# Three small moves in a tuned GEGLU kernel: paired 4 KB stores, an earlier first block of w_down, and late pieces of x through one PSUM bank

## The chip, the core and the metric

The kernel runs on one core of one Trainium2 chip. The metric is the device time of one execution in microseconds (us). Runs of the kernel before agree within 1.4 us in one set.

TensorE (PE in the profile, PEld for its weight loads), VectorE (DVE), ScalarE (ACT), GpSimd (POOL) and the queue that issues most DMAs (SPq) run side by side and wait for each other by semaphores.

## The reference

```python
x: (8, 1024, 1024)   w_gate, w_up: (1024, 4096)   w_down: (4096, 1024)   # float32
gate, up = x @ w_gate, x @ w_up
h = gelu_tanh(gate) * up
out = h @ w_down
```

## The kernel before

It works in float16 with float32 accumulators, in 8 passes of 1024 tokens. Each pass has a gate/up half and a w_down half. Passes 1 to 3 use a two-by-two fast matrix product with 512-column matmuls (7 products per pair of column blocks, 16 pairs to a pass); passes 4 to 8 use a larger scheme with 256-column matmuls, whose gate/up operands ("entries") are built once, in passes 2 and 3, and stored in HBM.

Some words that come again: the w_down half works through w_down in blocks of 1 MB, numbered from 0, with 32 matmuls for each. An "h product" is VectorE's product of gelu(gate) and up out of PSUM, which frees the accumulator banks. s3 is a buffer for one of the sums of h that the w_down half needs; an "s3 sum" fills a quarter of it. The "jam" is the stretch from 227 to 287 us in which DMA is full.

The parts that matter, cut:

```python
A_PARTS = ([8, 11, 12, 13, 16, 18, 22, 24, 25], [9, 10, 14, 15, 17, 19, 20, 21, 23])
# the sums that pass 2 and pass 3 make; entries_of() mixes in three plain copies each

def make_entry(p, q, e):               # in passes 2 and 3, 24 entries for each of 8 quads
    ...
    if n < 8: nc.scalar.activation(four(v), ..., COPY, scale=float(sign))   # plain: ScalarE
    else:     combine(four(v), op, a_node(p, q, a), a_node(p, q, b))        # sum: VectorE
    nc.sync.dma_start(out=wop[q, e // 2, :, e % 2], in_=v)                  # rows of 2 KB
...
            if i == NP - 1:                      # the last pair of pass 1
                at(1, load_d, p, 2 if p else 0)  # first block of w_down
...
        for r in range(4):                       # in the w_down half
            sums["P1", 0, r] = [("s3", "a11", "a21", SUB, r)]   # during block 0
            sums["P1", 1, r] = [("a21", "a21", "a22", ADD, r)]  # during block 1
...
        # first pair of pass 1: banks 5 and 7 hold pieces of x on their way out of the transpose
        x0_cast(0, 0, 1); x0_transpose(0, 0, 1, 5, act)
        x0_cast(0, 1, 1); x0_transpose(0, 1, 1, 7, dve)
        halves(1)
        product(1, 0, 1, 0)                      # accumulates in bank 5
        cast_first(1, 1, c0, dve)
        product(0, 1, 0, 0)
        ...
        cast_first(0, 1, c1)
        cast_first(1, 1, c1, dve)                # waits for the last landing of w_up
        sum_x(1); sum_w(0, 1, 0); sum_w(0, 1, 1); sum_x(2)
        outputs(1, 0); outputs(1, 1)
        sum_x(3); sum_w(0, 1, 2); sum_w(0, 1, 3); sum_x(4)
```

Of the kernel before, what the change touches and what calls it, by code (L numbers as in the profile page):

```python
# [11 lines left out]
ADD = mybir.AluOpType.add  # L12
SUB = mybir.AluOpType.subtract
# [21 lines left out]
A_SUMS = [  # L35
    (8, 'add', 5, 7), (9, 'sub', 6, 0), (10, 'add', 3, 5), (11, 'sub', 2, 0), (12, 'add', 4, 8), (13, 'sub', 1, 11),
    (14, 'sub', 1, 9), (15, 'add', 4, 10), (16, 'add', 4, 5), (17, 'add', 4, 9), (18, 'sub', 13, 3), (19, 'sub', 7, 14),
    (20, 'add', 2, 15), (21, 'add', 0, 1), (22, 'sub', 11, 8), (23, 'sub', 10, 9), (24, 'sub', 8, 1), (25, 'add', 6, 12),
]
# [8 lines left out]
A_ENTRIES = [  # L48
    (9, -1), (3, 1), (2, 1), (15, 1), (16, 1), (8, 1), (23, 1), (11, -1),
    (10, 1), (12, 1), (17, 1), (20, 1), (22, -1), (21, 1), (25, 1), (24, -1),  # L50
    (13, 1), (4, 1), (14, 1), (6, -1), (18, -1), (7, 1), (19, 1), (1, -1),
]
# [7 lines left out]
    (23, 22, 4, False),  # L60
]

A_PARTS = ([8, 11, 12, 13, 16, 18, 22, 24, 25], [9, 10, 14, 15, 17, 19, 20, 21, 23])

AFTER = {
    1: [('snap', 's8', 1)],
# [107 lines left out]
def kernel(  # L174
# [8 lines left out]
    nc = tc.nc  # L183
# [12 lines left out]
    NP = I // P // 2  # L196
    NQ = NP // 2
    G = MH // P
    FAST = 3
# [103 lines left out]
    def x0_cast(mh, gp, kh):  # L303
        nc.vector.tensor_scalar(
            x0_piece(x0_f16, 2 * mh + gp, kh), x0_piece(x0_f32[mh], gp, kh), XSC, None, MUL
        )

    def x0_transpose(mh, gp, kh, b, copy):
        h = x0_piece(x0_f16, 2 * mh + gp, kh)
        ps = ps_all[:, b].bitcast(FP16).rearrange("p (k m) -> p k m", m=MQ)  # L310
        o = xq[f"b{kh + 1}{mh + 1}"][:, :, gp * MQ : (gp + 1) * MQ]
        for k in range(KH):
            for t in range(2):
                nc.tensor.transpose(
                    ps[:, k, t * P : (t + 1) * P], h[:, t, k * P : (k + 1) * P], identity
                )
        copy(o, ps)
# [47 lines left out]
        xc[:, j * 1024 : (j + 1) * 1024] for j in range(8, 12)  # L365
    ]
    turn = [0]

    def four(v):
        return v.rearrange("p (w k n) -> p w k n", w=2, k=KH)  # L370
# [7 lines left out]
    def make_entry(p, q, e):  # L378
        n, sign = A_ENTRIES[e]
        v = place[q, n] = places[turn[0] % len(places)]  # L380
        turn[0] += 1
        if n < 8:
            nc.scalar.activation(four(v), a_node(p, q, n), COPY, scale=float(sign))
        else:
            _, op, a, b = A_SUMS[n - 8]
            combine(four(v), op, a_node(p, q, a), a_node(p, q, b))
        nc.sync.dma_start(out=wop[q, e // 2, :, e % 2], in_=v)

    def entries_of(part):
        sums = [n for n, _, _, _ in A_SUMS if n in A_PARTS[part]]  # L390
        plain = [n for n, _ in A_ENTRIES if n < 8][3 * part : 3 * part + 3]
        nodes = []
        for j, n in enumerate(sums):
            nodes.append(n)
            if j % 3 == 1:
                nodes.append(plain[j // 3])
        ids = [n for n, _ in A_ENTRIES]
        return [ids.index(n) for n in nodes]



# [49 lines left out]
    def half_block(v):  # L451
        lo, hi = slice(0, HH), slice(HH, 2 * HH)
        return (
            wd_half[0][:, :, lo], wd_half[1][:, :, lo], wd_t[1], wd_t[0],
            wd_half[0][:, :, hi], wd_half[1][:, :, hi], wd_half[0][:, :, lo],
        )[v]
# [71 lines left out]
    def d_place(p, k):  # L528
        if p == 0:

            return (4, 2, 3, 5, 4, 5, 4)[k // 2]
        return order[0][k % 6]

    def d_chunk(p, k):
        if p == 0 and k % 2:
            return half_block(k // 2)
        o = 4096 * d_place(p, k)
        return rg[:, o : o + 4096].rearrange("p (n h) -> p n h", n=8)

# [149 lines left out]
    def gate_up_one(p):  # L689
        unit_steps = {}  # L690
        if p in UNITS_ONE:
            free = deque(xc[:, j * 512 : (j + 1) * 512] for j in range(32, 38))
            free.append(spare)
            for u, s0, ds in UNITS_ONE[p]:
                load, fs = wd_unit(u, xc[:, 12288:16384], free)
                unit_steps[s0] = load
                for k, f in enumerate(fs):
                    unit_steps[s0 + 36 + ds * k] = f
        for i in range(NP):
            q, e = divmod(i, 2)  # L700
            extra = {k: [] for k in range(1, 15)}

            def at(k, f, *a):
                extra[k].append(lambda: f(*a))

            if p == 0 and i == 0:
                first_pair()
                continue
            if p == 0:
                if e == 1:  # L710
                    at(13, load_raw, p, q + 2)
                if 11 <= i < 15:
                    at(7, half_load, 0, 2 * (i - 11))
                if i >= 14:
                    at(4, half_load, 1, 4 * (i - 14))
                    at(6, half_load, 1, 4 * (i - 14) + 2)
                for n in range(4):

                    s0 = 28 * n + 72
                    for ds, f, a in (  # L720
                        (0, wd_load, (n, 0)), (2, wd_load, (n, 1)),
                        (4, wd_load, (n, 2)), (6, wd_load, (n, 3)),
                        (22, wd_sums, (0,)), (23, wd_sums, (1,)),
                        (24, wd_sums, (2,)), (25, wd_sums, (3,)), (26, wd_store, (n,)),
                    ):
                        pr, k = divmod(s0 + ds - 1, 14)
                        if pr == i:
                            at(k + 1, f, *a)
            elif i == 0:
                at(1, load_raw, p, 1)  # L730
            elif e == 1:

                at(13, load_raw, p, q + 2)

            ks = (3, 5, 7, 9) if e == 0 else (11, 12, 13, 14)
            for n, k in enumerate(ks):
                at(k, sum_w, p, i + 1, n)

            if FAST - 2 <= p < FAST:
                for j, n in enumerate(entries_of(p - FAST + 2)):  # L740
                    if j // 6 == e:
                        at(2 * (j % 6) + 2, make_entry, p, q, n)
            if (p, i) in ((0, 2), (FAST - 1, 13)):
                at(8, cast_x, p + 1)
            for k in range(14):
                if 14 * i + k in unit_steps:
                    at(k + 1, unit_steps[14 * i + k])
            if i == NP - 2:
                order[0] = [0, 1, 4, 2, 3, 5] if p % 2 == 0 else [2, 3, 4, 0, 1, 5]
                if p:  # L750
                    at(2, load_d, p, 0)
                    at(3, load_d, p, 1)
            if i == NP - 1:
                at(1, load_d, p, 2 if p else 0)
            second = p == 0 and i == 1
            pair(p, i, extra, SEQ0 if second else SEQ, AFTER0 if second else AFTER1)

# [149 lines left out]
    def down(p):  # L907
# [26 lines left out]

        sums = {}
        for r in range(4):
            sums["P1", 0, r] = [("s3", "a11", "a21", SUB, r)]
            sums["P1", 1, r] = [("a21", "a21", "a22", ADD, r)]
            sums["P2", 0, r] = [("a11", "a21", "a11", SUB, r)]
            sums["P6", 0, r] = [("a12", "a12", "a11", SUB, r)]  # L940

# [315 lines left out]
    def first_pair():  # L1257
# [3 lines left out]
        def product(mh, kh, w, j, c=full):  # L1261
            for k in range(KH):
                nc.tensor.matmul(
                    ps_all[:, bank[mh, j, w], c],
                    raw(0, 0)[:, w, kh * KH + k, j * P : (j + 1) * P],
                    xq[f"b{kh + 1}{mh + 1}"][:, k, c],
                    start=(kh == 0 and k == 0 and c.start == 0),
                    stop=(kh == 1 and k == KH - 1),
                    skip_group_check=True,
                )  # L1270
# [43 lines left out]
        for c in (lo, hi):  # L1314
            for j in range(2):
                product(1, 0, 0, j, c)
        x0_cast(0, 0, 1)
        x0_transpose(0, 0, 1, 5, act)
        x0_cast(0, 1, 1)
        x0_transpose(0, 1, 1, 7, dve)  # L1320
        halves(1)
        product(1, 0, 1, 0)
        cast_first(1, 1, c0, dve)
        product(0, 1, 0, 0)
        product(0, 1, 0, 1)
        x0_cast(1, 0, 1)
        x0_transpose(1, 0, 1, 7, act)
        x0_cast(1, 1, 1)
        product(0, 1, 1, 0)
        product(0, 1, 1, 1)  # L1330
        x0_transpose(1, 1, 1, 7, dve)
        outputs(0, 0)
        outputs(0, 1)
        for w in range(2):
# [2 lines left out]
        nc.gpsimd.tensor_copy(mark, staging0(1, 0)[:, 0, 256:257])  # L1337
        load_raw(0, 1)
        for c in (lo, hi):
            for w, j in ((0, 0), (0, 1), (1, 0)):  # L1340
                product(1, 1, w, j, c)
        for kh in range(2):
            product(1, kh, 1, 1)
        cast_first(0, 1, c1)
        cast_first(1, 1, c1, dve)
        ps_free.clear()
# [61 lines left out]
```

## Time and profile before

| | before |
|---|---|
| median, three runs | 2254.71 us |
| span of the profiled run | 2252.9 us |
| TensorE idle in the span | 7.7 us |
| single waits of TensorE in its list | 6, together 4.3 us, the last at 279 us |

The prediction shows the list of waits and the chain. Beside them, three stretches are needed. A timeline has the start in us, the duration, engine, line, operation, output and inputs, shape and count, and in brackets the idle time ahead and who ended it.

TensorE in the first pair: a wait of 0.65 us for ScalarE's copy out of bank 5.

```profile
15.54 1.06 PE L314 MATMUL ps<-identity,h_a 128*128 128x128 f16 x16
17.25 2.10 PE L1263 MATMUL ps<-x_b,ring 128*128 128x512 f16 x9 [0.65 <-ACT x_b L317]
```

VectorE at the beginning of the w_down half of pass 1: sums of s3 and half-sums of w_down (L461), one on the heels of the other.

```profile
214.59 2.35 DVE L932 TENSOR_TENSOR h_s<-h_a,h_a 128x2048 f16<-128x2048 f16 x2
216.86 1.21 DVE L461 TENSOR_TENSOR x_sums<-x_sums 128x2048 f16<-128x2048 f16 x1
218.00 1.21 DVE L932 TENSOR_TENSOR h_a<-h_a,h_a 128x2048 f16<-128x2048 f16 x1
```

The issuing queue ahead of the last wait: four DMA transposes of the next x, then the load of block 10 of w_down, for which TensorE waits.

```profile
259.64 11.07 SPq L255 DMA_TRANSPOSE x_b<-x_half  x4
270.81 0.53 SPq L544 DMA_DIRECT2D ring<-wd_ops  x1
```

### The profile page before, as it was taken

The numbers are of one execution on the slowest core, as the hardware profiler recorded it, in microseconds if no ns is written. First come the engines' busy times: TensorE is split into PE (matmuls) and PEld (weight loads), VectorE is DVE, ScalarE is ACT, GpSimd is POOL, SyncE is SP. The second block draws the span as 40 slices with busy tenths as digits, with TensorE's granted clock in tenths as the row PEclk, the third lists the DMA queues.
The fourth block names the chain that finished last, engine by engine and source line by source line (L and its number), as shares of the span: only waits on it lengthen the run. The fifth ranks groups of instructions, "written<-read, shape, count | busy, mean of one in ns | idle before, by whom it ended". The sixth has DMA issues, their size and how long they took to land.

```text
span 2252.9 us, 42769 instructions
## 1 busy us (share of the span) xinstructions
PE 2245.2 (100%) x16616; PEld 1624.1 (72%) x16616; DVE 1560.6 (69%) x2189; ACT 956.4 (42%) x1863; POOL 680.6 (30%) x825
## 2 busy tenths in 40 slices
PE   9999999999999999999999999999999999999999
PEld 4444444444444445888888888888888888888888
DVE  6666458883588755777776677666776667866674
ACT  4443135651355622666125550356404653055520
POOL 1332013330133200555014550255402543044520
PEclk9999999999999999999999999999999999999999
DMA  9898969989999999999998999989999889988876
GB/s 243 164 209 216 288 180 242 262 267 289 247 227 249 279 311 348 328 350 363 302 337 278 316 300 321 321 270 324 307 327 316 286 308 318 318 315 275 283 289 232
DMA packets 309133, 642.46 MB, mean 285 GB/s; under 512 B 79104, under 2 KB 185344, under 8 KB 288384
## 3 DMA queue, kind: packets, MB, share of 16 engines
q1 hardware_dynamic: 254144, 566.57, 73.5%
q0 software_dynamic: 54784, 73.14, 19.3%
q8 instruction: 130, 2.13, 0.4%
q14 instruction: 75, 0.61, 0.1%
HBM read 574.36 MB, written 138.41 MB: 316 GB/s over the span
## 4 chain that ended last, share of the span: by engine, by line
PE 87%; DMA 2%; SPq 1%; DVE 0%; issue 0%; DVEq 0%
PE ps L857 40%; PE ps L1108 20%; PE ps L635 17%; PE ps L1000 10%; DMA wd_quads<-x_sums 1%; SPq L255 0%; DMA ring<-wd_ops 0%; PE ps L1130 0%; DVE x_sums L278 0%; DVE h_a L932 0%; DVE tmp L1140 0%; SPq L496 0%; DVEq L278 0%; SPq L544 0%
## 5 line engine op out<-in xcount | busy, mean ns | idle before, releaser
L857 PEld LDWEIGHTS <-ring 128*128 128x128 f16 x8320 | 814.1, 98 | 94.4
L834 POOL TENSOR_TENSOR h_a<-tmp 128x256 f16<-128x256 f32 x640 | 469.2, 752 | 839.1 <-ACT tmp L822 831.9
L857 PE MATMUL ps<-x_sums,ring 128*128 128x256 f16 x5760 | 655.8, 273 | 0.0
L819 DVE TENSOR_TENSOR tmp<-tmp,ps 128x512 f32<-128x512 f32 x640 | 414.3, 683 | 148.2 <-PE ps L857 100.7
L635 PEld LDWEIGHTS <-ring 128*128 128x128 f16 x2632 | 257.4, 98 | 311.9 <-issue 1.1
L804 ACT COPY tmp<-ps 128x512 f32<-128x512 f32 x520 | 304.5, 586 | 236.7 <-PE ps L857 164.4
L635 PE MATMUL ps<-x_sums,ring 128*128 128x512 f16 x1504 | 340.1, 379 | 0.6 <-DVE x_sums L267 0.4
L822 ACT ACTIVATE tmp<-tmp 128x256 f32<-128x256 f32 x640 | 264.3, 418 | 172.6 <-DVE tmp L817 79.2
L857 PE MATMUL ps<-x_b,ring 128*128 128x256 f16 x2560 | 305.6, 273 | 0.0
L817 DVE TENSOR_TENSOR tmp<-ps,tmp 128x512 f32<-128x512 f32 x240 | 165.4, 689 | 145.2 <-ACT tmp L804 99.9
L635 PE MATMUL ps<-x_b,ring 128*128 128x512 f16 x1128 | 259.3, 379 | 0.1
L661 POOL TENSOR_TENSOR h_a<-tmp 128x512 f16<-128x512 f32 x94 | 145.5, 1548 | 372.9 <-ACT tmp L659 265.6
L1108 PEld LDWEIGHTS <-h_a 128*128 128x128 f16 x2208 | 216.0, 98 | 25.0
L1000 PE MATMUL ps<-ring,h_a 128*128 128x512 f16 x1024 | 222.3, 379 | 0.7 <-DMA ring<-wd_ops 0.7
L1108 PE MATMUL ps<-ring,h_a 128*128 128x256 f16 x1888 | 212.6, 273 | 0.0
L1000 PEld LDWEIGHTS <-h_a 128*128 128x128 f16 x1152 | 112.7, 98 | 136.8 <-DMA ring<-wd_ops 1.2
L654 DVE TENSOR_TENSOR tmp<-ps,tmp 128x512 f32<-128x512 f32 x188 | 127.2, 684 | 113.7 <-ACT tmp L646 112.2
L1238 ACT ACTIVATE tmp<-ps 128x512 f32<-128x512 f32 x60 | 35.3, 598 | 362.5 <-PE ps L1108 274.5
L1171 DVE SCALAR_TENSOR_TENSOR tmp<-ps,tmp 128x512 f32<-128x512 f32 x119 | 80.4, 690 | 95.0 <-PE ps L1108 64.1
L360 DVE TENSOR_TENSOR ring<-ring 128x1024 f16<-128x1024 f16 x188 | 137.6, 745 | 10.5 <-DMA ring<-in_w_up_dram 6.2
L646 ACT COPY tmp<-ps 128x512 f32<-128x512 f32 x188 | 109.8, 586 | 78.5 <-PE ps L635 78.5
L1108 PE MATMUL ps<-ring,x_sums 128*128 128x256 f16 x1120 | 126.3, 273 | 0.0
(105 smaller groups left out, 1538.0 us busy)
## 6 DMA issues: line engine op xcount, KB each, us to landing
ring<-w_ops SPq DMA_DIRECT2D x480, 512.0 KB, 4.8
ring<-wd_quads SPq DMA_DIRECT2D x110, 1024.0 KB, 7.1
ring<-wd_ops SPq DMA_DIRECT2D x35, 1024.0 KB, 7.9
w_ops<-h_s SPq DMA_DIRECT2D x128, 256.0 KB, 6.7
out_dram<-tmp SPq DMA_DIRECT2D x127, 256.0 KB, 6.3
ring<-in_w_gate_dram POOLq DMA_DIRECT2D x23, 1024.0 KB, 10.4
ring<-in_w_up_dram POOLq DMA_DIRECT2D x23, 1024.0 KB, 18.0
wd_quads<-x_sums SPq DMA_DIRECT2D x131, 128.0 KB, 6.6
```

What stands on the lines that cost most here:

```text
L360: nc.vector.tensor_tensor(o, a, b, op)
L635: nc.tensor.matmul(ps(b, w), lhs[:, k], rhs[:, k, :], start=(first and k == 0), stop=(k == KH - 1), skip_group_check=True,)
L654: nc.vector.tensor_tensor(o, ps("b", w), o, ADD)
L661: nc.gpsimd.tensor_tensor(hq[TO[n]][:, i, :], tmp[:, t[n, 1]], tmp[:, t[n, 0]], MUL)
L804: nc.scalar.copy(tmp[:, t[o[1]]], ps_all[:, bank[o[2]]])
L817: nc.vector.tensor_tensor(d, b, a, SUB)
L819: nc.vector.tensor_tensor(d, a, b, ADD if o[4] == "add" else SUB)
L822: nc.scalar.activation(d, d, GELU, scale=GSC)
L834: nc.gpsimd.tensor_tensor(h, tmp[:, t[o[1]], MQ : 2 * MQ], g, MUL)
L857: nc.tensor.matmul(ps_all[:, bank[c], w * MQ : (w + 1) * MQ], lhs[:, w, k], rhs[:, k], start=(first and w == 0 and k == 0), stop=(k == KH ...
L1000: nc.tensor.matmul(ps_all[:, bank[b, g]], lhs[:, j, g * P : (g + 1) * P], dc[:, n, :], start=(first and j == 0), stop=(j == NP - 1), skip_ ...
L1108: nc.tensor.matmul(ps_all[:, bank[c], m * MQ : (m + 1) * MQ], lhs[:, j, m * P : (m + 1) * P], rhs[:, j, :], start=(first and j == 0 and m ...
```

## The change

Its intent, as one reads it from the diff: fewer and longer stores in passes 2 and 3; w_down's block 0 loaded into s3 while DMA is idle, so that the one ring place that it used is free for block 8; and product work for TensorE while a late piece of x is copied out of PSUM.

```diff
-A_PARTS = ([8, 11, 12, 13, 16, 18, 22, 24, 25], [9, 10, 14, 15, 17, 19, 20, 21, 23])
+A_PARTS = (
+    [16, 8, 11, 12, 22, 21, 25, 24, 13, 4, 18, 7],
+    [9, 3, 10, 23, 2, 15, 17, 20, 14, 6, 19, 1],
+)
 ...                                                   # make_entry: part 1
-        nc.sync.dma_start(out=wop[q, e // 2, :, e % 2], in_=v)
+        if turn[0] % 2 == 0 and e % 2 and made_last[0] == (q, e - 1):
+            ...                                         # both places of the pair
+            nc.sync.dma_start(
+                out=wop[q, e // 2], in_=v.rearrange("p (e n) -> p e n", e=2)
+            )
+        elif (e ^ 1) not in entries_of(0 if p < FAST - 1 else 1):
+            nc.sync.dma_start(out=wop[q, e // 2, :, e % 2], in_=v)
 ...                                                   # part 2
+        if p == 0 and k == 0:
+            return hf["s3"][:, 4096:8192].rearrange("p (n h) -> p n h", n=8)
 ...
             if i == NP - 2:
+                at(2, load_d, p, 0)
                 if p:
-                    at(2, load_d, p, 0)
                     at(3, load_d, p, 1)
-            if i == NP - 1:
-                at(1, load_d, p, 2 if p else 0)
+            if i == NP - 1 and p:
+                at(1, load_d, p, 2)
 ...
-            sums["P1", 0, r] = [("s3", "a11", "a21", SUB, r)]
+            late = p == 0 and r > 1
+            sums.setdefault(("P1", int(late), r % 2 if late else r), []).append(
+                ("s3", "a11", "a21", SUB, r)
+            )
 ...                                                   # part 3
+        product(1, 0, 1, 1)                            # bank 7
         x0_cast(0, 0, 1)
-        x0_transpose(0, 0, 1, 5, act)
         x0_cast(0, 1, 1)
-        x0_transpose(0, 1, 1, 7, dve)
+        x0_transpose(0, 0, 1, 5, dve)
         halves(1)
-        product(1, 0, 1, 0)
+        x0_transpose(0, 1, 1, 5, dve)
 ...                                                   # the next two pieces too go through 5, not 7
```

More of the change, by code (lines that the diff above doesn't have):

```diff
@@ L367 @@
     turn = [0]
+    made_last = [None]
     def four(v):
@@ L386, in make_entry @@
             combine(four(v), op, a_node(p, q, a), a_node(p, q, b))
-        nc.sync.dma_start(out=wop[q, e // 2, :, e % 2], in_=v)
-    def entries_of(part):
-        sums = [n for n, _, _, _ in A_SUMS if n in A_PARTS[part]]
-        plain = [n for n, _ in A_ENTRIES if n < 8][3 * part : 3 * part + 3]
-        nodes = []
-        for j, n in enumerate(sums):
-            nodes.append(n)
-            if j % 3 == 1:
-                nodes.append(plain[j // 3])
+        if turn[0] % 2 == 0 and e % 2 and made_last[0] == (q, e - 1):
+            k = (turn[0] - 2) % len(places)
+            v = hf["s3"][:, k * 1024 : (k + 2) * 1024] if k < 8 else xc[:, k * 1024 : (k + 2) * 1024]
+            nc.sync.dma_start(
[3 more added lines that the diff above has]
+            nc.sync.dma_start(out=wop[q, e // 2, :, e % 2], in_=v)
+        made_last[0] = (q, e)
+    def entries_of(part):
         ids = [n for n, _ in A_ENTRIES]
-        return [ids.index(n) for n in nodes]
+        return [ids.index(n) for n in A_PARTS[part]]
     def wd_load(q, t):
@@ L936, in down @@
         for r in range(4):
-            sums["P1", 0, r] = [("s3", "a11", "a21", SUB, r)]
-            sums["P1", 1, r] = [("a21", "a21", "a22", ADD, r)]
+            late = p == 0 and r > 1
+            sums.setdefault(("P1", int(late), r % 2 if late else r), []).append(
+                ("s3", "a11", "a21", SUB, r)
+            )
+        for r in range(4):
+            sums.setdefault(("P1", 1, r), []).append(("a21", "a21", "a22", ADD, r))
             sums["P2", 0, r] = [("a11", "a21", "a11", SUB, r)]
@@ L1326, in first_pair @@
         x0_cast(1, 0, 1)
-        x0_transpose(1, 0, 1, 7, act)
+        x0_transpose(1, 0, 1, 5, act)
         x0_cast(1, 1, 1)
@@ L1330, in first_pair @@
         product(0, 1, 1, 1)
-        x0_transpose(1, 1, 1, 7, dve)
+        x0_transpose(1, 1, 1, 5, dve)
         outputs(0, 0)
@@ L1339, in first_pair @@
         for c in (lo, hi):
-            for w, j in ((0, 0), (0, 1), (1, 0)):
+            for w, j in ((0, 0), (0, 1), (1, 1)):
                 product(1, 1, w, j, c)
         for kh in range(2):
-            product(1, kh, 1, 1)
+            product(1, kh, 1, 0)
         cast_first(0, 1, c1)
```

## The prediction

> **What bounds the kernel now.** I read the page, then TensorE's list of waits, then the chain of waits in order of time, then timelines of the stretches in which TensorE stops.
>
> From the page, and from the list of waits (engine and line of the waiter, what it waited for; us in total, times, longest):
>
> ```profile
> PE 2245.2 (100%) x16616; PEld 1624.1 (72%) x16616; DVE 1560.6 (69%) x2189; ACT 956.4 (42%) x1863; POOL 680.6 (30%) x825
> ```
>
> ```profile
> PE ps L1284 <- DVE h_s L1287: 1.6, 1, 1.6
> PE ps L314 <- DVE h_a L304: 0.7, 1, 0.7
> PE ps L1000 <- DMA ring<-wd_ops: 0.7, 1, 0.7
> PE ps L1263 <- ACT x_b L317: 0.7, 1, 0.7
> PE ps L635 <- DVE x_sums L267: 0.4, 1, 0.4
> PE ps L635 <- DVE ring L360: 0.2, 1, 0.2
> ```
>
> TensorE is idle for 7.7 us of 2252.9. Six single waits make 4.3 us of it, all before 280 us; the rest is mostly the tail. The chain (start us, duration us, what) goes on without a break from there:
>
> ```profile
> 270.81 8.35 DMA ring<-wd_ops
> ...
> 279.21 27.80 PE ps L1000 x128
> 307.01 193.39 PE ps L635 x896
> 500.39 96.69 PE ps L1000 x448
> 597.09 193.39 PE ps L635 x896
> ```
>
> 193.39 us over 896 matmuls is 215.8 ns for 512 columns, and the later 181.65 us over 1664 is 109.2 ns for 256. The list of waits from 307 us on is empty. So the reader is to see that only the first 307 us can become shorter; everything behind (some 1946 us) can only become longer.
>
> **What the skill says.** "TensorE: Matmul & The Clock Gate", section "Wait — 56ns, not 53.3ns?", gives 215.7 ns between warm matmuls of 512 columns and 55.6 ns for 128. The trace agrees (215.8; the transposes step by 56), so the matmuls themselves hold no slack. "Perfetto Trace Analysis", section "DMA Optimizations", says that DMAs under 2 KB carry an overhead and that 4 KB pieces help. In this trace a 2 KB packet took 90 ns and a 1 KB one 50, so the gain of larger packets is small here, and no matmul waits for these stores. "SBUF — State Buffer", section "Who interferes with whom", says that a VectorE instruction with two SBUF inputs contends with a GpSimd one that reads SBUF. The trace agrees: a 128x2048 sum took 2.29 us beside a GpSimd product and 1.22 without. "Perfetto Trace Analysis", section "Matmuls", wants groups of matmuls to rotate through PSUM banks so that an eviction overlaps the next group; the third part of the change does the opposite.
>
> **Part 1, stores in pairs of 4 KB rows (passes 2 and 3).** Before: 24 entries x 8 quads = 192 stores of 256 KB. After: of each part's 12 entries 10 form five adjacent pairs and two stay single, so 2 x 8 x 5 = 80 stores of 512 KB and 32 of 256 KB: 80 issues fewer, at 0.3 us of the issuing queue each. Nobody waits for them until pass 4. What it moves: pass 2 gets 10 sums and 2 plain copies per quad instead of 9 and 3, and all six entries of its even pairs become VectorE work (before: five). VectorE is already full there:
>
> ```profile
> 355.35:367.44 12.09, 12.09 (x58) 5.49 (x56) 12.09 (x17) 6.70 (x11) 4.66 (x4) 1.00 1.04 225
> ```
>
> (one pair; busy us of TensorE, weight loads, VectorE 12.09 of 12.09, ScalarE, GpSimd, then clock and DMA.) One sum more is 0.6 to 1.1 us before the two products that free the accumulators. The one that matters, the first h product, ends 1.3 us before the next pair's third product needs its bank in this worst pair (367.85, against 367.44 + 8 x 0.216 = 369.17), 1.7 to 2.4 us in the others. So I count 0 for part 1, with little to spare.
>
> **Part 3, the first pair.** Before, TensorE waits 0.65 us at 17.25 for a ScalarE copy of 1.01 us out of bank 5. After, from 15.54 us: a product of four matmuls (0.86) to 16.40; transpose 1 (8 x 56 ns) to 16.85; the VectorE copy starts 0.19 later and takes 0.69, to 17.73; transpose 2, from the same bank, 17.79 to 18.24; its copy to 19.12; next product at 19.18. Before, that product started at 17.25 + 0.86 = 18.11. Same work in both, so TensorE is **1.07 us later**: two waits of some 0.9 us in place of one of 0.65. That delay then meets slack:
>
> ```profile
> 26.80 3.89 PE L635 MATMUL ps<-x_b,ring 128*128 128x512 f16 x16
> 30.53 1.03 PE L635 MATMUL ps<-x_sums,ring 128*128 128x512 f16 x4
> 31.95 2.75 PE L635 MATMUL ps<-x_sums,ring 128*128 128x512 f16 x12 [0.40 <-DVE x_sums L267]
> 34.89 2.13 PE L635 MATMUL ps<-x_sums,ring 128*128 128x512 f16 x9 [0.19 <-DVE ring L360]
> ```
>
> Start-to-start steps above 216 ns here are 0.28 us at 28.80 (a ScalarE copy in PSUM), 0.56 at 31.95 and 0.35 at 34.89: 1.19 us. The last two hang on VectorE, which runs without a break from 27.61, and that start is a landing of w_up at 27.59, behind 8 MB of loads that the change doesn't touch (DMA share 0.99 from 3 to 28 us). So the product at 34.89 starts there as before if the shift is under 1.19. **Net 0, at worst +0.2.** By the same bound, saving the 0.65 altogether would also have given 0.
>
> **Part 2, the first w_down block a pair sooner.** It is loaded from about 187 instead of 197.41 us, a stretch where DMA is nearly idle (0.01 to 0.02 from 185 to 191), into half of s3. Before, it landed at 203.5, and TensorE needed it at 209.31: no wait there, so 0 directly. Block 8 no longer waits for the end of block 0 and is issued at about 210 instead of 216.41; it is needed at 264.56, so 0 again. The price: two of the four s3 sums on VectorE must wait until TensorE has read block 0 (216.3). Before, VectorE went from sum to sum, with both done at 216.94 and a second w_down half-sum at 218.0; after, it has finished what it may do at 215.8, and idles till 216.4. Adding up the listed sums (1.13 each, 0.34 for the small ones), the fourth small sum ends at 225.77 instead of 225.09: **+0.67 us**. Behind it, in order on the same queue, come two stores of 1 MB (226.09 and 226.88). With these a stretch begins in which DMA is full:
>
> ```profile
> 227.00:287.00 60.00, 59.33 (x276) 26.73 (x275) 23.72 (x35) 8.40 (x15) 1.81 (x2) 1.00 1.08 301
> ```
>
> (219 to 227 had a share of 0.49.) At the end of that jam stands the only wait of this stage: block 10, queued behind four DMA transposes of x (11.07 us of issue from 259.64), lands at 279.16, while TensorE was due at 278.37 (step 1052 - 216 = 0.84 us). If the jam starts up to 0.67 us later with the same bytes, and its two weight loads of 1 MB do not shift, block 10 lands 0.3 to 0.7 later: the wait grows from 0.84 to about 1.3. **+0.5 us.**
>
> Sum: 0 + 0.05 + 0.5 on 2254.71 gives 2255.3; I take a little off, as the change was surely made for a gain: **2255.1 us**.
>
> **Rivals.** (a) Sooner loading relieves the queue, and block 10 lands in time. For it: 1 MB leaves the neighbourhood of 216 to 221 us. Against it: that load was over before the jam began. It would give -0.84, some 2253.9. (b) Part 3 does what it seems meant for and TensorE gains 0.65 at 17.25. Against it: the copies are serial in one bank, and VectorE's landing at 27.59 takes any gain back; 2254.7, no change. (c) The extra VectorE sum in the even pairs of pass 2 overruns the 1.3 to 2.4 us and TensorE waits for a bank, 0.3 to 1 us in some of seven pairs: +1 to +4, up to 2259. For it: VectorE at 12.09 of 12.09, and sums stretched to 2 us by GpSimd; against it: one sum more fits on average, and odd pairs have 2 to 4 us free. (d) The jam is chaotic (a store lands 9 us after its issue, and VectorE waits for buffers that stores free), so block 10 may move by 1 us either way.
>
> **Range and chances.** The three runs before spread over 1.4 us. All effects are of that size: (a) at the low end less the spread is 2253.3, (d) or a little of (c) at the high end 2256.9. Range 2253.3 to 2256.9. Two per cent is 45 us, ten times the largest rival: faster 0.005, within 2% 0.99, slower 0.005.
>
> **What would show it.** Right: TensorE's list has two waits on VectorE for bank 5 near 17 and 18.5 us, of 0.7 to 0.9, and nothing left at 31.95; the first product after VectorE's third weight sum still starts at 34.9; block 0 is issued near 187; the wait for block 10 is above 0.8 us; the list is empty from 307 us on; that stretch takes 1946 us as before. Wrong: a wait for block 10 gone or under 0.5 us (a), waits of TensorE on VectorE between 307 and 500 us (c), or a start at 34.9 that moved by over 0.3 us, which would say that VectorE's landing isn't the bound there.

## The result

| | before | the change |
|---|---|---|
| median (range), 6 runs each | 2254.43 us (2253.45 to 2254.88) | 2254.68 us (2253.79 to 2255.3) |
| span of the profiled run | 2252.9 | 2252.7 |

The ratio is 1.0002, with a 95% interval of 0.9989 to 1.0014: the same.

The new list of TensorE's waits:

```profile
PE ps L1298 <- DVE h_s L1301: 1.6, 1, 1.6
PE ps L317 <- DVE h_a L307: 0.9, 2, 0.6
PE ps L1014 <- DMA ring<-wd_ops: 0.9, 1, 0.9
PE ps L317 <- DVE x_b L320: 0.8, 1, 0.8
PE ps L1277 <- DVE x_b L320: 0.8, 1, 0.8
PE ps L1277 <- ACT ring L343: 0.3, 1, 0.3
PE ps L643 <- DVE ring L363: 0.2, 1, 0.2
```

The 0.7 us behind ScalarE's copy is gone; two waits of 0.8 us behind VectorE's copies (x_b, L320) stand in its place, and the wait for block 10 (L1014) is still there. The first pair on TensorE:

```profile
15.69 0.61 PE L317 MATMUL ps<-identity,h_a 128*128 128x128 f16 x8
17.08 0.61 PE L317 MATMUL ps<-identity,h_a 128*128 128x128 f16 x8 [0.78 <-DVE x_b L320]
18.47 1.89 PE L1277 MATMUL ps<-x_b,ring 128*128 128x512 f16 x8 [0.78 <-DVE x_b L320]
```

In this profile the extra product of four begins at 14.82 us, so the product at 18.47 comes 3.65 us after it. In before, the same work began at 15.54 and reached that product at 17.25 + 0.86 = 18.11: 2.57 us. The first pair is 1.08 us longer on TensorE. A little later:

```profile
30.61 3.81 PE L643 MATMUL ps<-x_sums,ring 128*128 128x512 f16 x16
34.60 1.68 PE L643 MATMUL ps<-x_sums,ring 128*128 128x512 f16 x7 [0.19 <-DVE ring L363]
```

The product at 34.60 is the one at 34.89 in before. I call its start **the mark**: the first product on the third weight sum of pair 1. In both profiles it starts 7.30 us after the last landing of w_up (27.59 and 27.30 us). The 1.08 us have gone into the gaps ahead of it.

The chain from the last wait on:

```profile
271.33 7.76 DMA ring<-wd_ops
...
279.13 27.80 PE ps L1014 x128
306.94 193.39 PE ps L643 x896
500.32 96.69 PE ps L1014 x448
```

Behind 307 us it has the same durations as before, and the list of waits from 307 us on is empty again. The stores of part 1 did get fewer: 192 of 256 KB became 80 of 512 KB and 32 of 256 KB. The DMA packets of before and of the change:

```profile
DMA packets 309133, 642.46 MB, mean 285 GB/s; under 512 B 79104, under 2 KB 185344, under 8 KB 288384
```

```profile
DMA packets 297611, 642.44 MB, mean 285 GB/s; under 512 B 77824, under 2 KB 184064, under 8 KB 276864
```

**The span as a sum.** One table holds all 14 profiles. The clock column is the start of the first 512-column matmul that is followed within 230 ns, which tells when TensorE goes from 427 to 216 ns per matmul. (It is read from the spacing, because the clock that the profile prints is 1.00 in the slow stretch too, as in the first 5 us of before. Where transposes come first, they show the step up to 0.4 us earlier.) The wait column is the start-to-start step at block 10, less 216 ns. The last column is the span less the mark, less that wait, less waits behind 307 us (0.31 in p3_only, 21.4 in sums_twice).

| kernel | clock quick at | mark, after last landing of w_up | wait for block 10 | span | rest |
|---|---|---|---|---|---|
| before | 9.59 | 34.89, 7.30 | 0.84 | 2252.9 | 2217.2 |
| p1_only | 6.23 | 34.70, 7.31 | 0.84 | 2252.6 | 2217.1 |
| p2_only | 9.16 | 34.77, 7.30 | 1.37 | 2253.3 | 2217.2 |
| before_unwarmed | 11.46 | 34.72, 7.32 | 0 | 2251.8 | 2217.1 |
| the change | 5.85 | 34.60, 7.30 | 1.05 | 2252.7 | 2217.1 |
| p3_only | 6.16 | 34.68, 7.30 | 0.77 | 2252.9 | 2217.1 |
| after_unwarmed | 9.25 | 34.70, 7.30 | 1.05 | 2252.8 | 2217.1 |
| late_swapped | 10.81 | 35.35, 8.01 | 1.25 | 2253.6 | 2217.0 |
| sums_twice | 10.37 | 35.56, 7.91 | 1.43 | 2275.3 | 2217.0 |
| transposes_later | 5.95 | 34.65, 7.31 | 0 | 2251.7 | 2217.1 |
| late_by_twelve | 5.93 | 36.71, 9.30 | 0.77 | 2254.5 | 2217.0 |
| product_between | 5.99 | 34.62, 7.31 | 0 | 2251.7 | 2217.0 |
| xsums_early | 6.03 | 34.14, 6.69 | 0.54 | 2251.7 | 2217.0 |
| three_together | 10.22 | 34.34, 6.79 | 0 | 2251.4 | 2217.0 |

The rest is the same within 0.3 us in kernels whose spans differ by 24 us. So every span here is that rest plus the mark, plus the wait for block 10, plus what TensorE loses in pass 2. Each experiment is read in these columns; the timed medians differ by little more than their spread.

### The profile page after: what moved, and what is told of

It reads as the page before. It is cut to its first block, busy times and chain, and to the rows that moved or that the text cites. A ratio compares the mean times of both kernels' runs of the same rounds, so it can differ in the third digit from the quotient of the medians.

```text
span 2252.7 us, 42628 instructions
## 1 busy us (share of the span) xinstructions
PE 2244.0 (100%) x16616; PEld 1622.7 (72%) x16616; DVE 1560.8 (69%) x2190; ACT 954.1 (42%) x1862; POOL 677.1 (30%) x825
## 4 chain that ended last, share of the span: by engine, by line
PE 98%; DMA 1%; SPq 1%; DVE 0%; issue 0%; DVEq 0%
PE ps L866 40%; PE ps L643 25%; PE ps L1122 20%; PE ps L1014 13%; DMA h_a<-in_w_up_dram 0%; SPq L337 0%; DMA ring<-wd_ops 0%; SPq L301 0%; PE ps L1144 0%; DVE x_sums L270 0%; DVE ring L363 0%; DVE h_a L1290 0%; DVE ring L343 0%; DVE tmp L1154 0%; DVEq L1290 0%
## 5 line engine op out<-in xcount | busy, mean ns | idle before, releaser
L1014 PE MATMUL ps<-ring,h_a 128*128 128x512 f16 x992 | 215.3, 379 | 0.9 <-DMA ring<-wd_ops 0.9
L1014 PEld LDWEIGHTS <-h_a 128*128 128x128 f16 x1152 | 112.6, 98 | 137.1 <-DMA ring<-wd_ops 1.4
L363 DVE TENSOR_TENSOR ring<-ring 128x1024 f16<-128x1024 f16 x188 | 143.0, 769 | 11.4 <-DMA ring<-in_w_up_dram 7.0
```

The costliest lines, as they stand in the source:

```text
L363: nc.vector.tensor_tensor(o, a, b, op)
L1014: nc.tensor.matmul(ps_all[:, bank[b, g]], lhs[:, j, g * P : (g + 1) * P], dc[:, n, :], start=(first and j == 0), stop=(j == NP - 1), skip_ ...
```

## The experiments

Each kernel was timed beside the kernel before on the same chip. All but sums_twice have 1 in the interval of their ratio. All results were correct.

### Each part alone: p1_only, p2_only, p3_only

The edit is one part of the diff above, put into the kernel before.

> The kernel before with part 1 alone (other order of the entries, stores in pairs). My theory: nobody waits for these stores, and VectorE's extra sum in the even pairs of pass 2 stays inside the slack; time within 0.7 us of before (2254.4), no wait of TensorE after 307 us, smallest gap between the first h product and the matmul that needs its bank 1.2 us or more. Rival (VectorE overruns): waits of 0.3 to 1 us in some even pairs of pass 2, +1 to +4 us. Rival (4 KB packets relieve the queues so that something ends sooner): under 2253. Up to 307 us this kernel is the same as before, so its wait for block 10 also shows how far that wait varies by itself: 0.84 in the profile of before, 1.05 in that of the change.

Measured: 2253.77 us against 2254.92 (ratio 0.9995, interval 0.998 to 1.001), and no wait behind 307 us. The gap between the first h product of an even pair of pass 2 and the third matmul group of the next pair, which takes over its bank, was at least 1.32 us. So no wait, and no relief that reaches TensorE either.

> The kernel before with part 2 alone (first block of w_down into s3 a pair sooner, two s3 sums later). In the profile of the change VectorE did not idle as I had forecast, so my mended theory is: no effect; wait for block 10 between 0.7 and 1.1 us as in a kernel without the part, the step at 34.9 as in before (7.30 us after the last landing of w_up), time within 0.7 us of before. The theory on record: wait about 1.3 us, +0.5. Rival (a), the queue is relieved: wait gone, -0.8.

Measured: 2254.93 us against 2254.92 (0.9999, 0.9983 to 1.0016). The mark is where it was, and the wait for block 10 is 1.37 us, above my mended theory and where the theory on record had put it. One profile can't decide between the two; late_swapped and the other profiles take this up.

> The kernel before with part 3 alone (first pair). Theory: two waits of TensorE on VectorE for bank 5 of about 0.78 us each in place of one of 0.65; TensorE 1.08 us later at the next product (3.65 us from the start of the extra product of four, against 2.57 from the start of the transposes in before), and yet the first product on the third weight sum starts 7.30 us after the last landing of w_up, as in before: net 0. Rival: the delay is carried on, the step is 1 us later against the landing and the time +1. Wait for block 10 as in before, 0.7 to 1.1.

Measured: 2254.67 us against 2254.92 (0.9998, 0.9983 to 1.0013). The two waits are there, 0.78 us each, and the mark lies 7.30 us behind the landing. The theory holds in this profile.

This one, which has pass 2 as in before, also held a surprise: the chain leaves TensorE once in pass 2.

```profile
442.28 0.61 DVE tmp L654
...
442.91 0.28 ACT tmp L659
...
443.45 1.04 ACT h_s L383
444.49 0.48 ACT tmp L646
...
445.01 55.41 PE ps L635 x256
```

A plain copy of an entry on ScalarE (L383) held up a PSUM snapshot (L646), and TensorE lost 0.31 us. But that copy was itself late because VectorE was: from 429.85 to 442.89 us the chain lies on VectorE almost without a break, and the h products of the pair before came 1.4 us later, counted from the start of the pair, than in before. The first of them had only 0.17 us to spare. So the order of entries that the change replaces can itself make TensorE wait. It did so in one of four profiles that have it; none of nine with the new order (sums_twice left out) had such a wait.

### The order of the two late s3 sums: late_swapped

```diff
-            sums.setdefault(("P1", int(late), r % 2 if late else r), []).append(
+            sums.setdefault(("P1", int(late), 3 - r if late else r), []).append(
```

In the change VectorE never idled at this place:

```profile
213.17 2.35 DVE L467 TENSOR_TENSOR x_sums<-x_sums 128x2048 f16<-128x2048 f16 x2
215.44 1.21 DVE L941 TENSOR_TENSOR h_s<-h_a,h_a 128x2048 f16<-128x2048 f16 x1
216.58 1.21 DVE L941 TENSOR_TENSOR h_a<-h_a,h_a 128x2048 f16<-128x2048 f16 x1
```

> The change, with its two late s3 sums in the other order: the one that overwrites the last rows of block 0 first. It has to wait for the very last matmul on block 0, so VectorE should idle 0.6 to 0.9 us here, which is the idle time that my prediction had put into the change itself. What follows tells whether the second half of that step was right: if the jam of the DMA queue starts as much later and block 10 lands later, the wait for block 10 grows from about 1.0 to 1.3 to 1.7 us and the time by 0.3 to 0.7; if the landing is set by something else, the wait stays between 0.8 and 1.1.

```profile
216.90 1.23 DVE L941 TENSOR_TENSOR h_s<-h_a,h_a 128x2048 f16<-128x2048 f16 x1 [0.67 <-issue]
```

Measured: VectorE idles 0.67 us, as expected, and the first 1 MB store of the jam is issued 17.53 us after the start of the w_down half; it is 16.78 in every other profile, to the hundredth. The wait for block 10 is 1.25 us. Its landing, counted from the same start, is 70.27 us. In the other profiles that leave its place in the queue alone it was 69.86, 69.86, 69.79 and 68.62 without part 2, and 70.07, 70.39, 68.55, 69.56, 69.79, 70.45 and 70.07 with it. One profile with 0.75 us more can't be told from a spread of 1.9 us, so whether a later jam makes block 10 land later stays open. What the columns do show is that part 2 isn't clear of that spread: the means of the two sets are 69.53 and 69.84. In all these profiles block 10 is issued 61.0 to 62.3 us after that start, and it lands 6.8 to 9.2 us after its issue; what sets this second time was not found.

The timed median was 2255.67 us against 2254.92 (1.0003, 0.9988 to 1.0018). In its profile the mark, too, came 0.7 us late, before any edit of this kernel could act.

### The place in the queue: transposes_later

```diff
-                    if nb == 0 and g == 0 and p + 1 < NPASS:
+                    if nb == (p == 0) and g == 0 and p + 1 < NPASS:
```

> The change, with the four DMA transposes of x issued behind the load of block 10 in pass 1, not ahead of it. Theory: block 10 is late only because it stands behind these transposes in the issuing queue; it is now issued near 258 to 260 us, lands by 270, the wait (1.05 us in the change's profile) is gone and the time is 0.8 to 1.1 us shorter. Rival: the queue is full anyway and block 10 lands as late, or block 12 takes its place behind the transposes and is waited for: no gain.

The issuing queue, which is to be compared with that of before:

```profile
259.30 0.40 SPq L552 DMA_DIRECT2D ring<-wd_ops  x1
259.74 14.00 SPq L258 DMA_TRANSPOSE x_b<-x_half  x4
```

Measured: block 10 landed at 267.08 us, 12 us sooner, nobody waited for it or for block 12, and the span is 2251.7. The median was 2253.53 us against 2254.12 for before (0.9997, 0.998 to 1.0014): the right direction, but too small for the runs to settle. That the wait comes from block 10's place behind four transposes, and not from the amount of data in the queue, is shown by the landing; the missing wait alone would not show it, since it was 0 by chance in two other profiles.

### Who holds the start: product_between, xsums_early, late_by_twelve

product_between lets the extra product cover the first of the two copies:

```diff
-        product(1, 0, 1, 1)
         x0_cast(0, 0, 1)
 ...
         halves(1)
+        product(1, 0, 1, 1)
         x0_transpose(0, 1, 1, 5, dve)
```

> The change, with the extra product of four matmuls put between the two transposes that share bank 5, so that it covers the first copy. TensorE reaches the next product about 0.78 us sooner (one wait left of two). Theory: no gain, because VectorE, held by the last landing of w_up, is the bound: the first product on the third weight sum still starts 7.3 us after that landing, and the saved 0.78 us comes back as waits just before it. Rival: TensorE's start counts, and the step is 0.5 to 0.8 us sooner against the landing.

```profile
31.68 2.75 PE L643 MATMUL ps<-x_sums,ring 128*128 128x512 f16 x12 [0.15 <-DVE x_sums L270]
34.62 2.56 PE L643 MATMUL ps<-x_sums,ring 128*128 128x512 f16 x11 [0.19 <-DVE ring L363]
```

Measured: one of the two waits is gone, and the mark is 7.31 us behind the landing, as ever. The saved time came back ahead of it. Its span of 2251.7 would look like a gain of 1 us over the change; that is the wait for block 10, which happened to be zero in this profile. The median is 2254.07 us against 2254.12.

xsums_early gives VectorE two sums to do ahead of the cast that waits for the last landing:

```diff
         cast_first(0, 1, c1)
+        sum_x(1)
+        sum_x(2)
         cast_first(1, 1, c1, dve)
 ...
-        sum_x(1)
         sum_w(0, 1, 0)
         sum_w(0, 1, 1)
-        sum_x(2)
```

> The change, with two sums of x (1.13 and 1.22 us) put on VectorE ahead of the cast that waits for the last landing of w_up, into the 2.35 us in which it idles. Theory: VectorE's chain behind the landing is 2.35 us shorter, TensorE no longer waits for it, and the first product on the third weight sum starts 6.7 to 6.8 us after the landing (TensorE's own pace, 7.30 less the waits of 0.19 and 0.35), so 0.5 us are gained. Rival: the bound isn't VectorE's chain: 7.3 as before.

```profile
24.96 1.22 DVE L270 TENSOR_TENSOR x_sums<-x_b,x_b 128x2048 f16<-128x2048 f16 x1
26.21 1.23 DVE L270 TENSOR_TENSOR x_sums<-x_b,x_sums 128x2048 f16<-128x2048 f16 x1
27.47 0.69 DVE L343 CAST ring<-h_a 128x1024 f16<-128x1024 f32 x1
```

Measured: the sums fill the hole exactly, the cast starts with the landing (27.44), and the mark comes 6.69 us after it, 0.61 less than in the change. The median is 2253.69 us against 2254.12 (0.9996, 0.9982 to 1.0011). So the chain landing, cast, sums was the bound; without it TensorE's own pace is.

late_by_twelve delays TensorE by 12 idle matmuls:

```diff
         product(0, 1, 0, 1)
+        for _ in range(12):
+            nc.tensor.matmul(ps_all[:, 5], warm_w, warm_x, start=True, stop=True)
         x0_cast(1, 0, 1)
```

> The change, with 12 idle matmuls of 512 columns (2.59 us) on TensorE in the first pair. Theory: the waits of 0.19 and 0.35 us behind VectorE take up 0.54 and the rest stays: the first product on the third weight sum starts 9.3 to 9.4 us after the last landing of w_up. For block 10: if its landing is tied to TensorE's progress (the jam in front of it begins with work that follows TensorE), the wait stays at 0.8 to 1.1 us and the time grows by about 2.0; if the landing is set by the DMA queues alone, the wait vanishes and the time grows by about 1.0.

Measured: the mark is at 9.30 us, so 2.00 of the 2.59 us came through. The wait for block 10 stayed, 0.77 us, and the median is 2256.24 us against 2254.12. Block 10's landing moves along with TensorE; the wait is no cushion in which a delay of the start could vanish.

### The slack in pass 2: sums_twice

```diff
-            combine(four(v), op, a_node(p, q, a), a_node(p, q, b))
+            for _ in range(2 if p == FAST - 2 and e in entries_of(0)[:6] else 1):
+                combine(four(v), op, a_node(p, q, a), a_node(p, q, b))
```

> The change, with each of the six VectorE sums of an even pair of pass 2 computed twice into the same place (the result stays right). Theory of the slack in pass 2: the first h product now has 1.64 to 2.65 us to spare before the matmul that needs its bank; five more sums of 0.6 us or more (3.0 us and up) ahead of it overrun that, and TensorE waits in most of the eight even pairs, 0.4 to 1.5 us each: +3 to +10 us in all, with waits between 307 and 500 us in the list. It shows that part 1's single extra sum used up some of a real limit. Rival: no such limit here: no wait, time as the change.

The list of waits from 300 us on:

```profile
PE ps L644 <- DVE tmp L663: 9.6, 11, 0.9
PE ps L644 <- DVE h_a L681: 6.3, 7, 1.2
```

Measured: 2276.5 us against 2254.85 (1.0094, 1.0079 to 1.011), double the most that I had expected. Behind 307 us TensorE loses 21.4 us from start to start; the list, which counts from modelled ends, has 16.7 with a third line of 0.8. The limit is real, but I had reckoned pair by pair. The odd pairs didn't empty VectorE's backlog: 48 extra sums at 0.6 us or more are at least 29 us, and VectorE had 193.4 - 158.9 = 34.5 us free in that half of the change. With some of them stretched, VectorE would have become the bound of the pass; this is reckoned, not tested apart. The run shows that a limit is there, not what part 1's one sum uses of it.

### The late clock: before_unwarmed, after_unwarmed

Both leave out the first seven idle matmuls (`warm(7)`).

> The kernel before without its first seven idle matmuls, so that TensorE's step from 427 to 216 ns for a 512-column matmul comes late (in the profiles so far it came at 5.9 to 6.2 us in seven kernels and at 9.2 to 10.8 in five, by chance of the execution). Question: does part 3 cost time when that step is late? With the change's first pair the first product on the third weight sum was 7.30 us after the last landing in the early profiles, but 8.01 and 7.91 in two late ones. Theory: with the first pair of before there is 1.08 us more to spare, so this kernel stays near 7.30, or, if the step comes so late that TensorE is the bound here too, lies 0.7 to 1.1 us under its sister. Rival: the late clock hides it equally, both the same.

> The change without its first seven idle matmuls. Theory: TensorE is the bound in the first pair, so part 3's 1.08 us are no longer hidden: the first product on the third weight sum comes 8 us or more after the last landing of w_up, 0.7 to 1.1 us more than in the sister kernel if the clock steps up at the same time in both, and the kernel is 0.5 to 1 us slower than it. Rival: 7.3 in both, same time.

Measured: 2254.3 us (0.9999, 0.9986 to 1.0013) and 2254.99 us (1.0001, 0.9989 to 1.0014), both against 2254.86. The quick clock came at 11.46 us in the first and at 9.25 us in the second, so the pair didn't meet under the same clock, and my forecast of 8 us or more for the second missed. Yet the two profiles are of use. The sister with the first pair of before reaches 7.32 us even at 11.46, and there TensorE has no gap left ahead of the mark; the one with the new pair reaches 7.30 at 9.25, and has none left either. I take it that each is just at its limit, so that the limits lie 2.2 us of slow clock apart. A slow microsecond costs TensorE half of its work (427 ns against 216), so this is 1.1 us of work: the 1.08 us by which part 3 lengthened the first pair. From 9.25 on, the new pair should lose half of every further microsecond: 0.56 us at 10.37 and 0.78 at 10.81. The two late profiles show 0.61 and 0.71. That fits, but it rests on one profile for each point.

### A version under both: three_together

It has the edits of transposes_later, product_between and xsums_early at once.

> The change with three of the edits at once: transposes of x behind block 10, the product between the two transposes, and two sums of x ahead of VectorE's last cast. Theory: no wait for block 10 (-1.0 us), and TensorE's wait behind VectorE gone; a ScalarE copy in PSUM that hangs on the landing before the last becomes the next bound, so the start-up gives 0.6 to 0.8 us. Together 1.5 to 1.9 us under the change, some 2252.9, and 1.3 to 1.7 under the kernel before; the interval will hardly tell it from 1.

Measured: 2253.18 us against 2254.85 (0.9994, 0.9982 to 1.0007), span 2251.4. The wait for block 10 and the one behind VectorE are gone, and the mark is at 6.79 us although the clock came late (10.22). It is the shortest profile, but by the interval it can't be called faster.

## Why the prediction was right

The forecast was 2255.1 us, in a range of 2253.3 to 2256.9, with 0.99 on "within 2%"; 2254.68 us was measured. That was right for its main reason: only the first 307 us could yield anything, and there the change touched small waits that others would take over. The number itself owes something to luck. The 0.05 us in its sum is not derived, the +0.5 us of part 2 had no cause (below), and 0.2 us were taken off because a change is surely made for a gain. A range of 3.6 us around runs that spread over 1.4 would also have held rivals (a), (b) and (d), so the time tests none of the steps. The signs do, but two of them came true loosely: the wait for block 10 was above 0.8 us (1.05) without the reason given, and the product at 34.9 moved by 0.29 us, just under the 0.3 allowed, since the landing ahead of it had moved as much. Block 0 was issued at 184.31 us, not near 187. Step by step:

- **Nothing behind 307 us.** Shown: the rest is 2217 us in all profiles, with the losses in pass 2 of p3_only and sums_twice taken off.
- **Part 1 counts 0.** Shown by p1_only. The step "One sum more is 0.6 to 1.1 us before the two products" holds where no sum is stretched (in the pairs from 379 and 403 us on the gap fell from 2.25 and 2.24 us to 1.59 and 1.73), but not for the smallest gap, which it meant to bound: that one grew. The chain gives the ends of matmuls, so the pair that the prediction read began 0.16 us sooner than it took it to, and its 1.3 us were 1.15. Counted from the starts, the smallest gap in an even pair of pass 2 was 1.15 us in before, 0.52 in p2_only, 0.66 in before_unwarmed and 0.17 in p3_only, and 1.32 to 1.40 in the nine profiles with the new order (sums_twice left out). Of the 70 sums of this half in before, 11 took over 0.9 us; of the 77 in the change, 4. The stretched ones that I looked at in before (at 358.8, 365.5 and 370.8 us) lie beside GpSimd products; why the new order has 4 to 10 of them and the old one 9 to 12 was not tested. Rival (c), a wait in pass 2 behind a late VectorE, turned up only in a kernel with the old order, and by way of ScalarE.
- **Part 3, TensorE 1.07 us later.** Measured: 1.08, with two waits of 0.78 us where I had said some 0.9.
- **Part 3, net 0 by VectorE's landing.** Shown by p3_only, and from both sides by product_between and xsums_early. This is where the gain sought in the first pair went: TensorE wasn't the bound there, so neither losing 1.08 us nor saving 0.78 moved the mark. "At worst +0.2" was mis-sized. I had reckoned with the clock of the one profile at hand. With a late clock the cost is 0.6 to 0.7, seen in two profiles; by the same half-a-microsecond reckoning I estimate 1.1 at 11.4 us, which no profile shows. How often a timed run has the late clock isn't in its time.
- **Part 2, VectorE idles until block 0 is read: +0.67 us.** Failed. VectorE idled 0, and the fourth small sum ended 15.79 us into the w_down half in all 13 profiles but late_swapped, with part 2 or without it. I let the sum wait for all of block 0. By the layout it overwrites only four of the block's eight slices, and TensorE's last group was past those when the sum started at 215.44. late_swapped, which touches the last slices first, has the forecast idle time.
- **Part 2, block 10 lands 0.3 to 0.7 later: +0.5 us.** With that its premise is gone. What the profiles show instead is a wait that varies between 0 and 1.4 us in kernels that do the same thing there. An effect of part 2 of a few tenths either way is not excluded. Rival (a), a relieved queue, is not borne out: the wait is no smaller with part 2. Rival (d), chance, describes best what was seen.

## What to carry to other kernels

Before shortening a wait, find the next thing that the same engine will wait for, and from what event that one is counted: here everything up to 34.6 us was counted from one landing, and two sums moved ahead of it brought TensorE 0.61 us nearer to it, which the rearrangement of banks did not. When the expected effect is under the spread of the runs, split the profile's span into a few named terms and look at those; a span that improves by chance in one term (product_between) is then not mistaken for a gain. Look at what a load that is wanted soon stands behind in its queue: here issuing it ahead of four DMA transposes made it land 12 us sooner.

## What the Trainium skill lacked or had wrong

- "TensorE: Matmul & The Clock Gate", section "What you observe", gives the step to the quick clock at around 4 us of sustained activity, "±500ns run-to-run". With the same opening of seven idle matmuls (the first at 1.59 us), seven of twelve kernels here had the quick clock by 6.23 us and five not until 9.16 to 10.81. In the change it was there by 5.46 us, in late_swapped a matmul at 10.13 was still slow: 4.7 us apart, where the page's band is 1 us wide. The activity here has gaps between its bursts, so it isn't the sustained one of the page.
- The same page, section "Part 4: PE-mode transpose", says some 275 ns per 128x128 transpose in one kernel and that the quick clock doesn't engage for them. Here one lasts 219 ns by the profile's modelled ends, and eight in a row start 56 ns apart once other matmuls have brought the quick clock, 107 before. Whether transposes alone would bring it was not tried.
- "Perfetto Trace Analysis", section "DMA Optimizations", says that going from "2KB → 4KB or 8KB" can dramatically improve throughput. In the gate/up halves of passes 2 and 3 a packet of 2 KB took 90 ns on average in before and one of 4 KB 166 in the change: some 7% less time for the same bytes, and none of it reached TensorE.
- Small tiles apart, no page gives how long DMA transposes from HBM hold an issuing queue. Four of them, 512 KB each, held it for 10 to 14 us, 4 to 7 of these for the first alone. In all 14 profiles the first ended 0.1 to 0.3 us before the last transfer issued ahead of it landed (264.5 and 264.7 us in before). The load behind the four came up to 1.4 us late.
